# Which half of a split weight unit begins 64 bytes further: the high part instead of the low part

## The chip, the cores and the metric

The kernel runs on one core of one Trainium2 chip. The metric is the device time of one execution in microseconds (us). A core has a matrix engine (PE; its weight loads are listed apart as PEld), a vector engine (DVE), a scalar engine (ACT), GpSimd (POOL) and SyncE (SP), which issues the DMAs here. They run side by side and wait for one another through semaphores. SBUF is the working memory with 128 partitions, PSUM the memory into which PE accumulates.

## What is computed

Two layers on an input of 256 tokens by 1024 features, all in float32. Each layer is a half-weighted gated feed-forward block (FFN, 2816 hidden features), a mixer, and a second such block; an RMS norm stands ahead of each and behind each. The mixer of the first layer joins a convolution branch with a state-space branch, that of the second is an attention over three dilated windows.

```python
def swiglu(u, w1, w2):
    gate, up = jnp.split(u @ w1, 2, axis=-1)
    return (jax.nn.silu(gate) * up) @ w2
...
for i in range(DEPTH):
    g = norm_g[i]
    h = h + 0.5 * rms_norm(swiglu(rms_norm(h, g[0]), ffn_w1[i, 0], ffn_w2[i, 0]), g[1])
    u = rms_norm(h, g[2])
    ...  # m = conv_ssd_mixer(u, ...) for i = 0, dilated_attention_mixer(u, ...) for i = 1
    h = h + rms_norm(m, g[3])
    h = h + 0.5 * rms_norm(swiglu(rms_norm(h, g[4]), ffn_w1[i, 1], ffn_w2[i, 1]), g[5])
```

## The kernel before

**Weights in units.** The host cuts all weights into units of 128 partitions by 2048 float32 numbers, 1 MB each, in the order of their use. `prefetch` brings a unit into a buffer of the kind `raw` by one DMA (the first two by four), three units ahead of its use, and `split` makes two parts of it, in pieces of 512 columns: ACT writes the high part `hi` (the number rounded to the format fp32r, in which PE runs at its full rate) into a buffer of the kind `wh`, then DVE, or GpSimd for a few units, writes the low part `lo` = `raw` - `hi` into a buffer of the kind `wl`. There are four buffers each of `raw`, `wh` and `wl`. Activations are split likewise, into tiles `x` (transposed activations, both parts in one tile) and `s` (gated hidden features, one tile for each part).

**Three products.** A float32 product is made of three fp32r ones: high by high, high by low, low by high. A matmul has a stationary operand, of 128 columns, which PEld loads, and a moving operand of up to 512 columns, which streams through the array. In the profile an entry such as `w<-x,wh` names the PSUM tile that is written and the tiles that are read, without saying which is stationary.

There are three uses of a unit, and `unit(inner)` is told by `inner` how its 2048 columns are divided:

- `inner` 512 (`tok_major`): eight blocks of 128 features by 512 columns, over two units. The activation `x` is stationary, the weights move.
- `inner` 1024 (`acc_pairs`, for the second FFN product and the output projections): two blocks of 128 rows by 1024 columns. The activation (`s` or `x`) is stationary, the weights move.
- `inner` 256 (`by_parts`, `feat_major`): eight blocks of 128 features by 256 columns. Here the weights are stationary, 128 columns at a time, and the activation `x` moves.

`by_parts` makes one feature-major block in one PSUM bank of two halves. For each of eight blocks of features it issues a pair: the high weights against both parts of `x` at once (512 columns), then the low weights against the high part (256 columns, into the first half of the bank):

```python
nc.tensor.matmul(ps, w[0], x, start=kb == 0, stop=False)
nc.tensor.matmul(ps[:, 0, :], w[1], x[:, 0, :], start=False, stop=kb == KB - 1)
```

Nine of the eleven chunks of every FFN's first product go through it, and most of the attention's projections. `feat_major`, in the hybrid mixer, issues three matmuls of 256 columns for each block: high weights by high `x`, high weights by low `x`, low weights by high `x`.

**Order of the work.** The kernel is first recorded as a list of operations; `schedule` then lays them out on the engines with the costs in `cost` and the handovers between engines, gives each tile one of its kind's buffers, and `issue` emits them in that order. Costs go by engine, operation, sizes and types; addresses do not enter.

**Where buffers lie.** Before anything is issued, `lay_out` places the SBUF buffers. First come those whose size is a multiple of 512 bytes, in the order of first use, then those of the kinds with a margin; behind each of the latter, small tiles are put until its size with them reaches a multiple of 512 bytes as nearly as they can. A kind with a margin has `LINE` = 16 more columns (64 bytes) than its tiles need, and a tile's `shift` says at which column of its buffer it begins:

```python
return self.real[:, self.shift : self.shift + self.cols] if self.kind.margin else self.real
```

A matmul or a split refers to a tile through a `View`, and `placed` turns it into an address when the operation is issued; a shift therefore holds for every operation that writes or reads that tile. So far `wl` is the kind with the margin, and a unit with `inner` 256 has its low part shifted by 64 bytes. A weight unit that moves is not shifted.

Of the kernel before, what the change touches and what calls it, by code (L numbers as in the profile page):

```python
# [166 lines left out]
class View:  # L167


    def __init__(self, buf, ap, path=()):  # L170
        self.buf, self.ap, self.path = buf, ap, path
# [30 lines left out]
LINE, LINES = 16, 512  # L202
# [47 lines left out]
class Recorder:  # L250
# [11 lines left out]
    def kind(self, pool, name, count, psum=False, margin=0):  # L262
        self.kinds[name] = Kind(pool, name, count, psum, margin)
# [291 lines left out]
class Kernel:  # L555
    def __init__(self, ctx, tc, x, weights, w_dt, gains, chan, heads, dt_bias, consts, out):
        self.tc, self.nc = tc, Recorder(tc)
        self.weights, self.gains = weights, gains
        self.x, self.out = x, out
        self.n = 0  # L560
        self.next_unit = 0
        self.use_unit = 0
        self.units = {}
        self.bg = []
        nc = self.nc
        sb = ctx.enter_context(tc.tile_pool(name="sb", bufs=1))
        ps = ctx.enter_context(tc.tile_pool(name="ps", bufs=1, space=PSUM))
        kind = lambda name, count: nc.kind(sb, name, count, margin=LINE if name == "wl" else 0)
        kinds = {"raw": RAW_BUFS, "wh": W_BUFS, "wl": W_BUFS, "g": 2, "junk": 2}
        for name, count in {**kinds, **SB_BUFS, **{f"m{n}": count for n, count in SMALL.items()}}.items():  # L570
            kind(name, count)
        for name, count in PS_BUFS.items():
            nc.kind(ps, name, count, psum=True)
        self.kind = kind

        self.h = [self.keep(f"h{t}", [P, D]) for t in range(NT)]
        self.ident = self.keep("ident", [P, P])
        self.order = self.keep("order", [P, 2, P])
        self.consts = consts
        self.gain0 = self.keep("gain0", [P, KB])  # L580
        self.mhalf = self.keep("mhalf", [P, 1])
        nc.gpsimd.memset(self.mhalf, -0.5)
        self.mean = self.keep("mean", [P, P])
        nc.gpsimd.memset(self.mean, 1.0 / D)
        self.chan = self.keep("chan", [P, N_CHAN])
        self.heads = self.keep("heads", [P, 2, 16])
        self.dt_bias = self.keep("dtb", [16, 1])
        self.in_small = (chan, heads, dt_bias, w_dt)
# [46 lines left out]
    def unit(self, inner):  # L635
        i = self.use_unit
        self.use_unit += 1
        self.prefetch(i + 1 + AHEAD)
        hi, lo = self.units.pop(i)

        lo.buf.shift = LINE if inner == 256 else 0
        r = lambda a: a.rearrange("p (k n) -> p k n", n=inner)
        return r(hi), r(lo)

# [27 lines left out]
    def feat_major(self, ps, xT, unit, blk):  # L672
        hi, lo = unit
        for kb in range(KB):
            w = tuple(a[:, kb, blk * P : (blk + 1) * P] for a in (hi, lo))
            x = self.xb(xT, kb)
            mm = self.nc.tensor.matmul
            mm(ps, w[0], x[0], start=kb == 0, stop=False)
            mm(ps, w[0], x[1], start=False, stop=False)
            mm(ps, w[1], x[0], start=False, stop=kb == KB - 1)  # L680

    def by_parts(self, xT, unit, blk, bank, out, scale=1.0):

        nc = self.nc
        hi, lo = unit
        ps = self.ps([P, 2, SEQ], bank)
        for kb in range(KB):
            w = tuple(a[:, kb, blk * P : (blk + 1) * P] for a in (hi, lo))
            x = xT[kb // 2][:, kb % 2]
            nc.tensor.matmul(ps, w[0], x, start=kb == 0, stop=False)  # L690
            nc.tensor.matmul(ps[:, 0, :], w[1], x[:, 0, :], start=False, stop=kb == KB - 1)
        nc.scalar.activation(out, ps[:, 1, :], AF.Copy, scale=scale)
        if scale == 1.0:
            nc.vector.tensor_tensor(out=out, in0=ps[:, 0, :], in1=out, op=ALU.add)
        else:
            nc.vector.scalar_tensor_tensor(out=out, in0=ps[:, 0, :], scalar=scale, in1=out, op0=ALU.mult, op1=ALU.add)

    def acc_pairs(self, acc, lhs, unit, kk, start, stop, halves=(0, 1), **kw):
        hi, lo = unit
        for hf in halves:  # L700
            c = slice(hf * 512, (hf + 1) * 512)
            self.mm3(acc[hf], lhs, (hi[:, kk, c], lo[:, kk, c]), start, stop, **kw)
# [734 lines left out]
```

## Time and profile before

| | |
|---|---|
| time, median of 3 runs | 1083.91 us (1083.85 to 1084.6) |
| time of the profiled execution | 1082.94 us |
| its span, first to last instruction | 1081.2 us |
| granted TensorE clock, mean | 0.999 |
| PE busy | 1065.2 us (99%), 5822 matmuls |
| PEld busy | 903.8 us (84%), 5822 loads |
| DVE busy | 762.9 us (71%) |
| ACT busy | 656.4 us (61%) |
| read from HBM | 194.51 MB, 181 GB/s over the span |

The time is what the device needs for the whole execution, the span is what the profile sees of it. Every instruction carries the same line number (L475, where the recorder emits), so the rows are told apart by tile names. A row of the groups gives the operation, tiles, shape and count, then the busy time of the group in us, the mean duration of one in ns, and the idle time of the engine just before them. Matmuls overlap: the duration of one is longer than the distance to the start of the next, and it is the latter that adds up to the time of a stage.

### The profile page before, as it was taken

How to read it: one execution, taken by the hardware profiler on the slowest of the kernel's cores; microseconds unless marked ns; L12 is line 12 of the kernel's file. 1: busy time of each engine (PE TensorE's matmuls, PEld its weight loads, DVE VectorE, ACT ScalarE, POOL GpSimd, SP SyncE). 2: the span in 40 equal slices, each digit the busy share in tenths (PEclk: the TensorE clock that was granted, in tenths of full speed). 3: DMA queues.
4: the chain of work that ended last, by engine and by line, in shares of the span. 5: the costliest groups of instructions: out<-in, count | busy, mean ns of one | idle time of the engine just before them, and what ended most of it. 6: DMA issues, size and time to landing. Idle time of an engine off the chain costs nothing.

```text
span 1081.2 us, 15876 instructions
## 1 busy us (share of the span) xinstructions
PE 1065.2 (99%) x5822; PEld 903.8 (84%) x5822; DVE 762.9 (71%) x1572; ACT 656.4 (61%) x1449; POOL 147.3 (14%) x140
## 2 busy tenths in 40 slices
PE   7999999999999999999999999999999999999997
PEld 5888888888878888888888888888888788888886
DVE  5756666889999885765677656668688868576563
ACT  7745555787776664654565646556576756465452
POOL 2000000169896000000000000000000400000000
PEclk9999999999999999999999999999999999999999
DMA  9764465545324475546537465454745236554621
GB/s 335 283 211 178 178 202 188 164 149 195 118 92 147 190 272 195 195 159 230 175 137 273 162 228 176 175 195 145 254 158 187 98 118 214 196 195 163 227 79 39
DMA packets 30638, 196.58 MB, mean 182 GB/s; under 512 B 3680, under 2 KB 4576, under 8 KB 8032
## 3 DMA queue, kind: packets, MB, share of 16 engines
q1 hardware_dynamic: 30560, 195.57, 51.4%
q8 instruction: 45, 0.74, 0.3%
q14 instruction: 33, 0.27, 0.1%
HBM read 194.51 MB, written 1.05 MB: 181 GB/s over the span
## 4 chain that ended last, share of the span: by engine, by line
PE 93%; DVE 3%; ACT 2%; DMA 0%; issue 0%; SPq 0%; DVEq 0%; POOLq 0%; POOL 0%; ACTq 0%
PE w L475 38%; PE a L475 31%; PE t L475 12%; PE c L475 12%; DVE c L475 1%; DVE t L475 1%; ACT wh L475 1%; DMA raw<-in_weights 0%; ACT junk L475 0%; DVE s L475 0%; ACT c L475 0%; ACT t L475 0%; SPq L475 0%; DVE m L475 0%; DVE h L475 0%
## 5 line engine op out<-in xcount | busy, mean ns | idle before, releaser
L475 ACT ACTIVATE wh<-raw 128x512 fp32r<-128x512 f32 x712 | 405.4, 625 | 197.1 <-PE a L475 80.0
L475 DVE TENSOR_TENSOR wl<-raw,wh 128x512 fp32r<-128x512 f32 x640 | 412.1, 690 | 159.7 <-ACT wh L475 157.5
L475 PE MATMUL w<-x,wh 128*128 128x512 f32 (+1 forms) x864 | 266.4, 365 | 0.9 <-DVE pt L475 0.7
L475 PE MATMUL a<-wh,s 128*128 128x512 f32 x800 | 253.2, 391 | 0.0
L475 PE MATMUL w<-x,wl 128*128 128x256 f32 x752 | 210.9, 280 | 0.0
L475 PEld LDWEIGHTS w<-x,wh 128*128 128x128 f32 x864 | 154.6, 188 | 28.3 <-DVE pt L475 1.0
L475 PEld LDWEIGHTS a<-wh,s 128*128 128x128 f32 x800 | 150.0, 188 | 33.1 <-ACT s L475 0.9
L475 PE MATMUL w<-wh,x 128*128 128x512 f32 x512 | 167.1, 400 | 0.9 <-ACT x L475 0.8
L475 PE MATMUL a<-wl,s 128*128 128x512 f32 x400 | 156.6, 391 | 0.0
L475 PEld LDWEIGHTS w<-x,wl 128*128 128x128 f32 x752 | 142.9, 190 | 2.0 <-issue 0.9
L475 POOL TENSOR_TENSOR m<-m,mhalf 128x1 f32<-128x1 f32 x28 | 18.1, 647 | 801.3 <-DVE m L475 801.2
L475 PE MATMUL t<-x,wh 128*128 128x512 f32 x336 | 118.5, 392 | 0.0
L475 PE MATMUL c<-x,wh 128*128 128x512 f32 x336 | 118.5, 392 | 0.0
L475 PEld LDWEIGHTS w<-wh,x 128*128 128x128 f32 x512 | 96.0, 189 | 21.7 <-ACT x L475 1.6
L475 PE MATMUL w<-wl,x 128*128 128x512 f32 x256 | 101.9, 400 | 0.0
L475 POOL TENSOR_TENSOR wl<-raw,wh 128x512 fp32r<-128x512 f32 x72 | 90.6, 1305 | 28.1 <-ACT wh L475 27.9
L475 PE MATMUL t<-x,wl 128*128 128x256 f32 x336 | 94.0, 280 | 0.0
L475 PE MATMUL c<-x,wl 128*128 128x256 f32 x336 | 93.9, 280 | 0.0
L475 PEld LDWEIGHTS a<-wl,s 128*128 128x128 f32 x400 | 75.1, 188 | 14.7
L475 DVE TENSOR_TENSOR sg<-w,sg 128x256 f32<-128x256 f32 x72 | 30.5, 423 | 78.3 <-ACT sg L475 75.9
L475 ACT ACTIVATE sg<-w 128x256 f32<-128x256 f32 x96 | 36.7, 382 | 80.0 <-PE w L475 80.0
L475 PEld LDWEIGHTS c<-x,wh 128*128 128x128 f32 x336 | 63.1, 188 | 13.6
(176 smaller groups left out, 1202.0 us busy)
## 6 DMA issues: line engine op xcount, KB each, us to landing
raw<-in_weights SPq DMA_DIRECT2D x176, 1024.0 KB, 4.8
g<-in_gains SPq DMA_DIRECT2D x11, 512.0 KB, 5.3
raw<-in_weights SPq DMA_DIRECT2D x8, 256.0 KB, 6.2
h<-in_x SPq DMA_DIRECT2D x4, 256.0 KB, 3.1
out<-h SPq DMA_DIRECT2D x4, 256.0 KB, 2.0
g<-in_consts SPq DMA_DIRECT2D x3, 192.0 KB, 2.3
chan<-in_chan SPq DMA_DIRECT2D x1, 170.0 KB, 8.9
order<-in_consts SPq DMA_DIRECT2D x1, 128.0 KB, 8.9
```

The costliest lines, as they stand in the source:

```text
L475: o.ins = f(*[real(a) for a in o.args], **{k: real(a) for k, a in o.kw.items()})
```

## The change

The kind `wh` gets the margin in place of `wl`, and for a unit with `inner` 256 it is the high part that begins 16 columns (64 bytes) into its buffer, while the low part begins at column 0. All other tiles keep their place within their buffers; the buffers' own addresses are given out anew, since `wl` is now placed with the plain kinds and `wh` with those that have a margin.

```diff
-        kind = lambda name, count: nc.kind(sb, name, count, margin=LINE if name == "wl" else 0)
+        kind = lambda name, count: nc.kind(sb, name, count, margin=LINE if name == "wh" else 0)
...
-        lo.buf.shift = LINE if inner == 256 else 0
+        hi.buf.shift = LINE if inner == 256 else 0
```

## The prediction

> **What bounds the kernel now.** I read the page first, for the engine that sets the time.
>
> ```profile
> span 1081.2 us, 15876 instructions
> PE 1065.2 (99%) x5822; PEld 903.8 (84%) x5822; DVE 762.9 (71%) x1572; ACT 656.4 (61%) x1449; POOL 147.3 (14%) x140
> PEclk9999999999999999999999999999999999999999
> PE 93%; DVE 3%; ACT 2%; DMA 0%; issue 0%; SPq 0%; DVEq 0%; POOLq 0%; POOL 0%; ACTq 0%
> ```
>
> PE is busy for 99% of the span at a granted clock that never drops, and 93% of the chain that ended last is PE. So a nanosecond matters where a matmul starts a nanosecond later or earlier, and hardly anywhere else. The change moves bytes of the stationary weight units, so the second view is the groups of instructions by form: how many matmuls take such a unit as stationary operand?
>
> ```profile
> L475 PE MATMUL w<-x,wh 128*128 128x512 f32 x640 | 225.0, 393 | 0.0
> L475 PE MATMUL w<-x,wl 128*128 128x256 f32 x752 | 210.9, 280 | 0.0
> L475 PE MATMUL t<-x,wh 128*128 128x512 f32 x336 | 118.5, 392 | 0.0
> L475 PE MATMUL c<-x,wh 128*128 128x512 f32 x336 | 118.5, 392 | 0.0
> L475 PE MATMUL w<-x,wh 128*128 128x256 f32 x224 | 41.3, 285 | 0.9 <-DVE pt L475 0.7 <-DVE s L475 0.2
> L475 PE MATMUL a<-x,wh 128*128 128x256 f32 x96 | 17.5, 283 | 0.4 <-ACT v L475 0.4
> ```
>
> The 512-wide rows are the high products of `by_parts`: 640 + 336 + 336 = 1312. Each is followed by one 256-wide low product, so there are 1312 pairs. The 256-wide rows with `wh`, 224 + 96 = 320, are the two high products of `feat_major`; with one low product each two, that is 160 triples.
>
> What one pair costs is not its "mean ns" (matmuls overlap), but the distance from start to start. The chain of waits in order of time gives it; its columns are start us, us, what:
>
> ```profile
> 46.58 10.93 PE a L475 x48
> 57.50 5.55 PE w L475 x32
> ```
>
> The second row is 16 pairs in 5.55 us: 346.9 ns a pair, and 1312 x 346.9 ns = 455 us, 42% of the span. The first row is a run of 512-wide matmuls whose stationary operand is an activation and starts at the buffer's beginning, both parts: 10.93 / 48 = 227.7 ns each. Now the timeline of PE inside both runs (start us, us, instruction):
>
> ```profile
> 46.41 0.40 PE L475 MATMUL a<-wh,s 128*128 128x512 f32 x1
> 46.65 0.40 PE L475 MATMUL a<-wl,s 128*128 128x512 f32 x1
> 46.88 0.62 PE L475 MATMUL a<-wh,s 128*128 128x512 f32 x2
> 47.34 0.39 PE L475 MATMUL a<-wl,s 128*128 128x512 f32 x1
> 47.58 0.40 PE L475 MATMUL a<-wh,s 128*128 128x512 f32 x1
> ...
> 56.44 0.62 PE L475 MATMUL a<-wh,s 128*128 128x512 f32 x2
> 56.89 0.39 PE L475 MATMUL a<-wl,s 128*128 128x512 f32 x1
> 57.12 0.39 PE L475 MATMUL a<-wh,s 128*128 128x512 f32 x1
> 57.34 0.39 PE L475 MATMUL w<-x,wh 128*128 128x512 f32 x1
> 57.57 0.28 PE L475 MATMUL w<-x,wl 128*128 128x256 f32 x1
> 57.69 0.40 PE L475 MATMUL w<-x,wh 128*128 128x512 f32 x1
> 57.92 0.28 PE L475 MATMUL w<-x,wl 128*128 128x256 f32 x1
> 58.03 0.39 PE L475 MATMUL w<-x,wh 128*128 128x512 f32 x1
> 58.26 0.28 PE L475 MATMUL w<-x,wl 128*128 128x256 f32 x1
> 58.38 0.39 PE L475 MATMUL w<-x,wh 128*128 128x512 f32 x1
> ```
>
> Two things are to be seen. The plain 512-wide stream starts at (47.58 - 46.41) / 5 = 234 ns a matmul and ends at (57.34 - 56.44) / 4 = 225 ns; the whole run's 227.7 says that most of it is near 227. So the same instructions with the same addresses modulo a buffer run at 234 when they come out of a `by_parts` run and then settle. And a pair divides into 230 ns from high to low (0.23, 0.23, 0.23) and 117 from low to high (0.12, 0.11, 0.12). The load of the next stationary operand runs under each matmul: today the shifted low load under the long matmul, the unshifted high load under the short one. The change swaps the two.
>
> **The change part by part.** The planner's `cost` has no term for a margin or a shift, so the order, the instructions, the waits and the DMAs stay as they are, on all queues; only addresses change. There are four effects.
>
> (1) The buffers of `wh` grow by 64 bytes and those of `wl` shrink. `lay_out` starts every large buffer at the same remainder of 512 bytes and fills the rest of each enlarged one with small tiles; it does so with the other kind too. Price 0; below and above there is nothing to bound it by but the other prices.
>
> (2) ACT writes the high part, DVE or GpSimd reads it 64 bytes further on, and writes the low part at the beginning.
>
> ```profile
> L475 DVE TENSOR_TENSOR wl<-raw,wh x640: 676/684/1584, 8.9 to 1058.5; 128x512 fp32r<-128x512 f32 x160
> L475 ACT ACTIVATE wh<-raw x712: 612/622/718, 8.2 to 1057.8; 128x512 fp32r<-128x512 f32 x178
> ACT wh L475 <- PE a L475: 80.0, 37, 3.2
> ```
>
> The DVE row mixes shifted outputs (units used as stationary) with unshifted ones, and its shortest and median are 8 ns apart, so a shifted operand costs at most about 8 ns of 684. The cover is the prefetch: splits wait for a free buffer, that is for PE (80.0 us in 37 waits in the last row), not the other way round. Were the cover gone, 640 x 8 ns = 5 us would be the most. I take 0.
>
> (3) The triples, 160 of them, get two shifted loads instead of one. They stand in the hybrid stage, where the chain is not on PE; for the window from 224 to 260 us it says:
>
> ```profile
> by line: DVE c L475 44.9%; DVE t L475 32.4%; DVE s L475 9.6%; DVE m L475 3.8%; DVE cv L475 3.6%; ACT c L475 2.6%; DVE a L475 2.1%; PE w L475 1.1%; issue 0.7%
> ```
>
> DVE's long convolution sets the end there and hides the triples. Without that cover, 3 ns on each of 480 matmuls would be 1.4 us in either direction. I take 0.
>
> (4) The pairs. No row has an unshifted low load under the long `x` stream, or a shifted high load under a short matmul in a pair, so both halves are bounded by neighbours. From high to low, now 230: the unshifted load under a 512-wide stream took 227 settled and 234 unsettled. Lower end -3, upper end +4; the pair's alternation of long and short never gives a plain stream to settle in, nor a change of stream, behind which 234 was seen, so it lies between, and I take the middle, 230.5: +0.5. From low to high, now 117: the loads' own durations (min/median/max) bound it. The first row is of the window 225 to 259 us, where the low load runs under a 256-wide matmul, the others are of the whole span.
>
> ```profile
> L475 PEld LDWEIGHTS w<-x,wl x80: 189/192/192, 224.9 to 255.7; 128*128 128x128 f32 x80
> L475 PEld LDWEIGHTS c<-x,wl x336: 187/189/193, 43.6 to 1058.0; 128*128 128x128 f32 x168
> L475 PEld LDWEIGHTS c<-x,wh x336: 186/188/188, 43.5 to 1057.9; 128*128 128x128 f32 x168
> ```
>
> A shifted load takes up to 192 ns, an unshifted one 188. If the short matmul hides none of that, the step is +4. Whether it hides it, the triples show, start to start:
>
> ```profile
> 225.17 0.40 PE L475 MATMUL w<-x,wh 128*128 128x256 f32 x2
> 225.41 0.28 PE L475 MATMUL w<-x,wl 128*128 128x256 f32 x1
> 225.52 0.40 PE L475 MATMUL w<-x,wh 128*128 128x256 f32 x2
> ...
> 226.23 0.40 PE L475 MATMUL w<-x,wh 128*128 128x256 f32 x2
> ```
>
> (226.23 - 225.17) / 9 = 117.8 ns a matmul, although one in three has the 192 ns load under it; that is 0.8 above the pair's 117. So I take +0 here, with ends -1 (a shifted load that hurries the short step) and +4.
>
> The Trainium skill ("TensorE: Matmul & The Clock Gate", LDWEIGHTS) states that a weight load takes the number of its columns over 1.2, in ns, thus 107 for 128 columns; the same page gives a warm 256-wide matmul 256 / 2.4 + 2.5 = 109, an estimate from its figures. By these two the load is as long as the short matmul and the 4 ns would all be exposed: +5.2 us in place of 0. The triples' 117.8 do not bear that out, hence it is a rival and not the sum.
>
> Sum: +0.5 ns x 1312 pairs = +0.7 us, all else 0. The profiled execution took 1082.94 us, 1.74 more than its span, and the median of the runs shown is 1083.91, 0.97 above it. 1083.91 + 0.7 = 1084.6 us. 2.2 us (0.2%) is about what a measurement of this kernel can tell from no change; that is 1.65 ns a pair.
>
> **The rivals.** *A: the low load collides (slower).* Unshifted, it runs under the long matmul as in the unsettled stream, 234 for 230, and the alternation keeps it from settling. For it: the same 512-byte remainders as in the 234 ns rows. Against: that stream does settle within its run. Price +4 x 1312 = +5.2 us: 1089.1. It decides from 231.7 on.
>
> *B: the high load's last 4 ns show under the short matmul (slower).* For it: loads of 192 ns exist only where a shift is. Against: the triples' 117.8. Price between half (today only about half of the pairs' shifted loads are long, median 189) and all: +2 to +4 ns x 1312 = +2.6 to +5.2 us: 1086.5 to 1089.1. With A it would reach 1094.
>
> *C: the long step settles to the plain stream's 227 and the short one stays at 117 (faster, the other side).* For it: that stream's settled rows are the nearest unshifted loads under a 512-wide matmul. Against: their moving operand is a weight, not `x`. Price -3 x 1312 = -3.9 us: 1080.0. It decides from 228.3 downwards.
>
> That the change does nothing it says can be left out: the shift belongs to the buffer and is applied when instructions are issued, so the split writes where the matmuls read.
>
> **How the numbers follow.** My forecast, a pair within 1.65 ns of today's, gets 0.40; A 0.21, B alone 0.14, C 0.25. Hence slower 0.35, same 0.40, faster 0.25. The likeliest one's own range is 1081.7 to 1086.1. For 8 in 10 I go to C with its short step at -1 as well as its 3 ns, 4 x 1312 = 5.2 below the median: 1078.7, taken as 1079; and above to A with half of B, 6 x 1312 = 7.9 us: 1091.8, taken as 1092. Outside stay A with all of B and a settling faster than any row here.
>
> **What would show it.** In the profile after, 16 pairs in the chain of waits should again take 5.5 to 5.6 us. The load's durations should change places: `wh` loads of up to 192, `wl` loads of 188. From high to low near 230 confirms (4); 234 is A, 227 is C; from low to high of 119 to 121 is B. Splits should stay at 622 and 684 ns. Pairs at 340 or 353 ns would mean that the two steps depend on each other, so that bounding each by itself, as done in (4), was the error.

## The result, and the profile after

The changed kernel takes 1076.99 us (median of 4 runs, 1076.7 to 1077.57), the kernel before 1083.88 in the runs beside it: a ratio of 0.9938, 95% interval 0.992 to 0.9955. It is 0.6% faster. The forecast was 1084.6 us, no change, and the time lies below its range.

The page after:

```profile
span 1074.9 us, 15876 instructions
PE 1058.9 (99%) x5822; PEld 897.9 (84%) x5822; DVE 762.3 (71%) x1572; ACT 654.9 (61%) x1449; POOL 147.4 (14%) x140
PE 93%; DVE 3%; ACT 2%; DMA 0%; issue 0%; SPq 0%; DVEq 0%; POOLq 0%; POOL 0%; ACTq 0%
```

The span is 6.3 us shorter, PE's busy time too (1065.2 to 1058.9), with the same 5822 matmuls and the same shares in the chain. So the matmuls start closer together. The chain of waits in order of time (start us, us, what), after:

```profile
57.47 5.46 PE w L475 x32
62.93 2.72 PE t L475 x16
65.65 2.72 PE c L475 x16
68.37 5.46 PE a L475 x24
```

and the same stretch before:

```profile
57.50 5.55 PE w L475 x32
63.05 2.77 PE t L475 x16
65.82 2.77 PE c L475 x16
68.60 5.49 PE a L475 x24
```

A row of 32 is 16 pairs: 5.46 / 16 = 341 ns where it was 347; a row of 16 is 8 pairs: 2.72 / 8 = 340. A chunk of 32 pairs falls from 11.09 to 10.90 us. (A wide stream is a run of 512-wide matmuls in which the weights move, such as the row of 24.) Each FFN has eight such chunks behind its first wide stream of second products, four FFNs 32 of them: 32 x 0.19 = 6.1 us. The 24 wide streams between these chunks fall from 5.49 to 5.46 us each, some 0.7 us in all, and the pairs in other places lose about as much, as shown below; together that is nearly all of the gain. The timeline of PE after shows where in a pair:

```profile
57.31 0.40 PE L475 MATMUL w<-x,wh 128*128 128x512 f32 x1
57.55 0.28 PE L475 MATMUL w<-x,wl 128*128 128x256 f32 x1
57.66 0.39 PE L475 MATMUL w<-x,wh 128*128 128x512 f32 x1
57.89 0.28 PE L475 MATMUL w<-x,wl 128*128 128x256 f32 x1
58.00 0.39 PE L475 MATMUL w<-x,wh 128*128 128x512 f32 x1
58.23 0.28 PE L475 MATMUL w<-x,wl 128*128 128x256 f32 x1
```

After a first 0.24 the long step takes 0.23 each time and the short one 0.11. The starts in the trace, which has whole nanoseconds, give medians of 227 and 113 ns in this chunk, against 230 and 117 before: **both** steps became shorter. Not every run of pairs gained. The first chunk of an FFN starts behind transposes, not behind a wide stream; in all four FFNs it became slower, in the first 2.80 us for 8 pairs (350 ns) where it was 2.77 before, and so did most of the attention's pairs. Here is the first FFN's first chunk, after and before:

```profile
36.73 4.20 PE w L475 x24
40.93 2.80 PE t L475 x16
```

```profile
36.86 4.17 PE w L475 x24
41.03 2.77 PE t L475 x16
```

So the same instructions, with operands at the same remainders of 512 bytes, repeat with 340 ns in one run and 350 ns in another. Such a spacing, which holds from the start of a run to its end, is called a cycle below.

### The profile page after: what moved, and what is told of

The parts are those of the page before. It is cut to its first block, busy times and chain, and to the rows that moved or that the text cites. A ratio compares the mean times of both kernels' runs of the same rounds, so it can differ in the third digit from the quotient of the medians.

```text
span 1074.9 us, 15876 instructions
## 1 busy us (share of the span) xinstructions
PE 1058.9 (99%) x5822; PEld 897.9 (84%) x5822; DVE 762.3 (71%) x1572; ACT 654.9 (61%) x1449; POOL 147.4 (14%) x140
## 4 chain that ended last, share of the span: by engine, by line
PE 93%; DVE 3%; ACT 2%; DMA 0%; issue 0%; SPq 0%; DVEq 0%; POOLq 0%; POOL 0%; ACTq 0%
PE w L475 38%; PE a L475 32%; PE t L475 12%; PE c L475 12%; DVE c L475 2%; DVE t L475 1%; ACT wh L475 1%; DMA raw<-in_weights 0%; ACT junk L475 0%; DVE s L475 0%; ACT c L475 0%; ACT t L475 0%; SPq L475 0%; DVE m L475 0%; DVE h L475 0%
```

## The experiments

The theories are stated in the expectations, numbered from 1 to 5; the later ones came when the earlier had fallen. Each was timed beside the kernel before on the same chip; ratios are to it. The pairs are read from the second chunks of the first FFN, in the chain of waits between 57 and 70 us.

**No shift at all, and where the buffers lie.** Two kernels shift nothing; one keeps the margin on `wh`, the other on `wl`, so that their buffers lie as in the changed kernel and as in the one before.

```diff
-        hi.buf.shift = LINE if inner == 256 else 0
+        hi.buf.shift = 0
```

> Margin on wh as in the changed kernel, but no part of a stationary unit is shifted. Theory 1 (each step by itself: the cost of a matmul depends on whether the load under it begins 64 bytes off the moving operand's remainder; long step 227 ns over an unshifted load and 230 over a shifted one, short step 117 over an unshifted and 113 over a shifted one): pair 227 + 117 = 344 ns, 1312 x 4 ns = 5 us slower than the changed kernel, about 1082 us. Theory 2 (what matters is that the high and the low load lie apart from each other; the pair locks as a whole): pair about 350 ns, as in the changed kernel's runs that start behind a break, 13 us slower than the changed kernel, about 1090 us. Theory 3 (where the buffers lie, not the shift): about 1077 us.

> Margin on wl as in the kernel before, no part of a unit shifted. Theories 1 and 2: equal to the kernel with the margin on wh and no shift, within 2 us, because the placing of the buffers does not matter. Theory 3 (where the buffers lie): equal to the kernel before, about 1084 us, and 6 to 7 us slower than the one with the margin on wh.

They took 1091.75 us (ratio 1.0066, 1.0049 to 1.0082) and 1091.49 us (1.0067, 1.0052 to 1.0082). Margin on `wh`, then on `wl`:

```profile
42.71 2.77 PE t L475 x16
...
59.18 5.64 PE w L475 x32
```

```profile
58.14 5.64 PE w L475 x32
```

Both need 5.64 / 16 = 352.5 ns a pair. The placing of the buffers does nothing (theory 3 falls). Theory 1 falls too: its 227 + 117 gave 344. The time fits theory 2. The row at 42.71 is of the first chunk, and there this kernel without a shift takes 2.77 us for 8 pairs, as the kernel before does. So the spacing of the kernel before is found without any shift too; what is missing is one of 340 ns.

**Both parts shifted.** Margins on both kinds; an unused tile goes out to make room.

```diff
         hi.buf.shift = LINE if inner == 256 else 0
+        lo.buf.shift = hi.buf.shift
```

> Both parts of a stationary unit are shifted by 64 bytes (margins on both kinds; an unused tile and its memset are left out to make room, small tiles lie elsewhere). Theory 1 (each step by itself): long step 230, short step 113, pair 343 ns, 4 us slower than the changed kernel, about 1081 us. Theory 2 (apart from each other): same as no shift at all, about 350 ns a pair and 1090 us.

1091.76 us (1.0073, 1.0058 to 1.0088), and again:

```profile
58.10 5.64 PE w L481 x32
```

As slow as no shift; theory 1's 343 ns is off by 10. One part of the two has to be shifted, and not the other.

**How far.** The distance of the high part is changed, `LINE` from 16 columns (64 bytes) to 8, 24, 32, 48 and 64 columns.

```diff
-LINE, LINES = 16, 512
+LINE, LINES = 64, 512
```

> The changed kernel with 32 bytes in place of 64. If the two loads have to lie in different pieces of 64 bytes: partly as no shift, 347 to 353 ns a pair, 1084 to 1092 us. If any distance does it: 340 ns, 1077 us.

> The changed kernel with 96 bytes in place of 64. With the period of 128 bytes that 128, 192 and 256 showed, 96 is 32 on the other side of 64: if 64 is the best point and its sides are alike, about 351 ns a pair and 1089 us as with 32 bytes; if more than 64 is as good as 64, 340 ns and 1077 us.

> The changed kernel with 128 bytes in place of 64. Theory 2 (the distance of the high load from the low load decides) with a period of 128 bytes: as with no shift, 352.8 ns a pair and about 1091.7 us. With a period of 256 bytes: neither 0 nor 64; the high part lies as far ahead of the low part as behind it, so between the two kernels at the worst, 340 to 347 ns, 1077 to 1084 us.

> The changed kernel with 192 bytes in place of 64. Period 256 bytes: 192 ahead is 64 behind, so this is the kernel before in another place, 346.9 ns a pair and about 1084 us. Period 128 bytes: 192 is 64, so 340 ns and about 1077 us; the kernel before would then have to be explained by something else than the distance.

> The changed kernel with 256 bytes in place of 64. Theory 1 with a fine grain (any offset off the moving operand's remainder of 512 does it): 340 ns a pair, 1077 us. If the offset must be small, because the load is to begin just behind or ahead of the moving stream: 344 to 350 ns a pair, 1082 to 1090 us.

| bytes | time us | ratio (95%) |
|---|---|---|
| 32 | 1088.91 | 1.0045 (1.003 to 1.006) |
| 64 (the change) | 1076.99 | 0.9938 (0.992 to 0.9955) |
| 96 | 1084.04 | 1.0005 (0.9996 to 1.0014) |
| 128 | 1090.64 | 1.0059 (1.0042 to 1.0076) |
| 192 | 1077.1 | 0.9936 (0.9922 to 0.9951) |
| 256 | 1091.63 | 1.0069 (1.0054 to 1.0084) |

A chunk's first row for 32, 96, 128, 192 and 256 bytes, one kernel a fence:

```profile
58.59 5.62 PE w L475 x32
```

```profile
57.41 5.55 PE w L475 x32
```

```profile
59.01 5.62 PE w L475 x32
```

```profile
58.46 5.46 PE w L475 x32
```

```profile
58.09 5.64 PE w L475 x32
```

192 is as good as 64, 128 and 256 are about as bad as 0. What counts is the remainder of 128 bytes, and 64 is the best point tried; 32 and 96 would be alike if the two sides of 64 were; they are not (5.62 and 5.55). With this period, 64 ahead and 64 behind are the same distance, so theory 2 alone cannot tell the changed kernel from the one before. Something third must be in it.

**The moving operand's place.** The high part is shifted in every unit, also where the weights move and activations are stationary.

```diff
-        hi.buf.shift = LINE if inner == 256 else 0
+        hi.buf.shift = LINE
```

> The changed kernel with the high part shifted in every unit, also where it is the moving operand (inner 512 and 1024). Theory 2: the moving operand's place does not matter, so those 512-wide streams stay at 227 ns, the pairs at 340 ns, and the time at 1077 us. Theory 1 in its remaining form (place of the load against the moving operand): two in three of some 2060 wide matmuls change by 3 ns, 4 us either way.

1091.72 us (1.0073, 1.0058 to 1.0088):

```profile
46.65 11.20 PE a L475 x48
57.85 5.45 PE w L475 x32
68.74 5.59 PE a L475 x24
74.33 5.60 PE w L475 x32
...
85.53 5.60 PE a L475 x24
91.13 5.45 PE w L475 x32
```

The wide stream of 48 takes 11.20 / 48 = 233 ns a matmul where the kernel before has 10.93 / 48 = 228. No load was moved there, only two in three moving operands, so the place of the moving operand matters. The pairs, whose addresses are those of the changed kernel, need 340 ns behind one stream (5.45) and 350 behind the next (5.60), and 340 again behind a stream that is like that one (5.59 and 5.60). So these addresses allow both cycles. A cycle stays through a chunk, although its 32 pairs go through two units and several PSUM tiles; this speaks for the beginning of a run as what chooses, but what in the beginning it is, the runs do not show.

**The activations shifted instead.** Now `x`, the moving operand of the pairs, is shifted by 64 bytes as well, once in the kernel before (low part shifted) and once in the changed one.

```diff
-        return [self.slot([P, 2, 2, SEQ], F32R, "x") for _ in range(KB // 2)]
+        tiles = [self.slot([P, 2, 2, SEQ], F32R, "x") for _ in range(KB // 2)]
+        for v in tiles:
+            v.buf.shift = LINE
+        return tiles
```

> The kernel before (low part shifted) with every tile of x shifted by 64 bytes too (margins on wl and x, an unused tile and its memset left out). Against the moving operand x the high load is then 64 off and the low load is not, as in the changed kernel. Theory 4 (remainder modulo 128 of a load against the operand that moves above it: the long step wants the same remainder, the short step one 64 off): 340 ns a pair in the runs behind a wide stream. The wide streams with x stationary are now 64 off, as the ones in the kernel with the high part shifted everywhere, 233 for 227 ns: 864 x 6 ns = 5 us more; in all about 1082 us. Theory 5 (only the two loads against each other, high one ahead): 347 ns a pair as in the kernel before, about 1089 us.

> The changed kernel with every tile of x shifted by 64 bytes too. Against x the high load is then not off and the low load is, as in the kernel before. Theory 4: 347 ns a pair, and 5 us more in the wide streams with x stationary, about 1089 us. Theory 5: 340 ns a pair as in the changed kernel, about 1082 us with the wide streams' 5 us, 1077 without.

Low part and `x` shifted: 1079.53 us (0.996, 0.9945 to 0.9975). High part and `x` shifted: 1089.34 us (1.0052, 1.0035 to 1.0069). In this order:

```profile
30.05 5.60 PE w L484 x24
...
58.06 5.46 PE w L484 x32
```

```profile
29.51 5.60 PE w L484 x24
...
57.79 5.60 PE w L484 x32
...
798.46 5.55 PE w L484 x32
```

This settles it against theory 5; theory 4 has the right kernel short, but not the other one's 347 ns. With `x` shifted, the roles change over: shifting the low part now gives 340 ns, and shifting the high part gives 350. The distance of the two parts is the same in both; what differs is which load has the same remainder as the operand that moves above it. The pairs are short where the load under the long matmul has the same remainder as `x` and the load under the short one is 64 bytes off. The first row of each fence is a wide stream with `x` stationary, 24 in 5.60 us; before it was

```profile
29.40 5.48 PE w L475 x24
```

so there, too, 64 off costs 5 ns a matmul. That is a reason why the first of the two is not as fast as the changed kernel although its pairs are; theory 4's 1082 us was 2.5 us too high. The second has the offsets of the kernel before but repeats at 350 and not at 347 ns, except in some runs of the attention (the row at 798.46, 347 ns): this set of offsets, too, has more than one cycle.

The cycle of 340 ns belongs to one set of offsets alone. In the traces of the four kernels in which the high load is 64 bytes off `x` and the low load is not (the changed one, 192 bytes, the high part shifted in every unit, the low part and `x` shifted), runs of pairs settle at 340 ns. In the other eleven kernels no eight pairs in a row take less than 346 ns a pair.

**Half-way places.** `x` by 32 and the high part by 96 bytes, then `x` by 96 and the high part by 32. The high load stays 64 off `x`, the low one is 32 off on one side and on the other.

```diff
-            v.buf.shift = LINE
+            v.buf.shift = 8
...
-        hi.buf.shift = LINE if inner == 256 else 0
+        hi.buf.shift = 24 if inner == 256 else 0
```

> Tiles of x shifted by 32 bytes and the high part by 96. Against x the high load is 64 off as in the changed kernel, the low load 96 (32 on the other side), and in the wide streams the stationary x is 32 off the moving weights. Theory 4 with a grain of 64 bytes: the long step is neither same nor 64 off, so between 227 and 233 ns, and the short step stays at 113: 342 to 347 ns a pair; wide streams with x stationary between 227 and 233 ns. If 32 off were better than the same remainder, they would fall below 227 ns, which would open a way to a faster kernel.

> Tiles of x shifted by 96 bytes and the high part by 32. Against x the high load is 64 off, the low load 32, the stationary x of the wide streams 96 off. Theory 4: as with the roles of 32 and 96 exchanged, 342 to 347 ns a pair; wide streams with x stationary between 227 and 233 ns, below 227 if this offset is better than none.

1091.26 us (1.007, 1.0047 to 1.0093) and 1089.86 us (1.0055, 1.0033 to 1.0078):

```profile
29.22 5.60 PE w L484 x24
...
57.54 5.62 PE w L484 x32
```

```profile
29.92 5.61 PE w L484 x24
...
58.19 5.59 PE w L484 x32
```

5.62 and 5.59 us are 351 and 349 ns a pair, worse than the 342 to 347 expected. The long step's load is best at the same remainder, of the places tried; moving it by 32 either way loses the short cycle. The wide streams with `x` stationary say the same (the rows at 29 us): 5.60 and 5.61 us for 24, 233 to 234 ns a matmul, so 32 off costs as much there as 64 off. No kernel here is faster than the changed one by more than the intervals; the one with 192 bytes is its equal.

## Why the prediction was wrong

**The bound and the count held.** PE set the time, 1312 pairs were the main place of weight, and most of the gain is found in 1024 of them.

**(1), (2) and (3) held.** Where buffers lie was worth nothing (1091.75 against 1091.49 us without a shift). The splits stayed at 622 and, after, 685 ns:

```profile
L475 DVE TENSOR_TENSOR wl<-raw,wh x640: 677/685/1577, 8.9 to 1052.2; 128x512 fp32r<-128x512 f32 x160
L475 ACT ACTIVATE wh<-raw x712: 612/622/723, 8.3 to 1051.6; 128x512 fp32r<-128x512 f32 x178
```

The triples cost nothing, though the reason given covers only a part of them: the window from 224 to 260 us holds 289 of their 480 matmuls, and for some of the others PE is on the chain. One such stretch, 38 of their matmuls, took nearly the same before and after:

```profile
283.67 4.76 PE a L475 x38
```

```profile
281.91 4.74 PE a L475 x38
```

**(4) failed, and with it the sum.** Its step was to bound the long and the short step each by itself, from neighbouring streams, and to add. The forecast was +0.5 and 0 ns, the lower ends -3 and -1, a pair of 343; measured are -3 and -4, a pair of 340. (The unsettled 234 was read from rounded starts; whole nanoseconds give 232 for those five matmuls, which would have lowered the upper end and changed nothing else.) The long step did what rival C said, 227. The short step fell to 113, below the end of 116, with a shifted load under it; so rival B's price did not appear, nor the +5.2 us for all of the load's last 4 ns. The trace before had 113 ns, in 256-wide matmuls with loads of 16 columns, which had not been taken as an end; the timeline of PE before:

```profile
222.30 0.28 PE L475 MATMUL w<-x,wdtl 128*16 128x256 f32 x1
...
223.32 0.28 PE L475 MATMUL w<-x,wdtl 128*16 128x256 f32 x1
```

Nine matmuls start from the first row to the last: (223.32 - 222.30) / 9 = 113 ns. The deeper fault is the adding: with the steps as measured, the same rule gives 344 ns for no shift and 343 for both shifts, and both cost 353. The two steps repeat as one cycle. The prediction named 340 or 353 as the sign of just that, but gave it no chance.

**The loads' durations were a false guide.** Long loads were to move with the shift. In the hybrid stage they did, `wl` from 192 to 188 and some of `wh` to 192 (the first two rows, after, 223 to 257 us). In the pairs nearly all vanished (the last two, whole span):

```profile
L475 PEld LDWEIGHTS w<-x,wl x80: 187/188/189, 223.2 to 253.9; 128*128 128x128 f32 x80
L475 PEld LDWEIGHTS w<-x,wh x159: 186/188/192, 223.1 to 253.8; 128*128 128x128 f32 x159
...
L475 PEld LDWEIGHTS c<-x,wh x336: 186/188/189, 43.5 to 1051.6; 128*128 128x128 f32 x168
L475 PEld LDWEIGHTS c<-x,wl x336: 187/188/192, 43.6 to 1051.7; 128*128 128x128 f32 x168
```

The shifted `wh` load takes at most 189 ns under the short matmul. Nor does a load of 192 need a shift: in the kernel with the margin on `wl` and nothing shifted, loads of the hybrid stage have it too, while the kernel with both parts shifted, at 353 ns a pair, has nearly none (in this order):

```profile
L475 PEld LDWEIGHTS a<-x,wl x48: 188/192/192, 253.2 to 295.9; 128*128 128x128 f32 x48
```

```profile
L481 PEld LDWEIGHTS c<-x,wl x336: 187/188/190, 44.2 to 1066.5; 128*128 128x128 f32 x168
```

So the loads' durations tell neither the shift nor the cycle, and rival B's premise, that 192 exists only where a shift is, was wrong.

**Rival A's long step came in a part of the pairs.** In this kernel's first chunk in the first FFN the long step has a median of 233 ns in the trace, and in the second chunk of the kernel without a shift (margin on `wh`) one of 236, although the low load under it lies at the same remainder as in the runs at 227. So the low load's place does not set the long step by itself. In the wide streams 233 ns appear once load and moving operand are 64 off. That is the opposite of the condition that was given for A: the same remainder is the good place under the matmuls of a wide stream.

**What was not foreseen at all** is that one set of addresses has several cycles, so that a part of the pairs, as in the first chunk above, became slower. How far the time falls therefore depends also on how many pairs find the cycle of 340 ns: most of them here, but only about a third with the high part shifted in every unit, where the pairs have the same offsets. Why there are several cycles, what chooses among them, and which machinery sets the 128 bytes, the runs do not show.

## What to carry to other kernels

Where PE sets the time and weight loads alternate with matmuls, the byte address of a stationary operand, taken modulo 128 against the operand that moves while it is loaded, is worth trying: here 340 to 353 ns a pair, 1.4% of the whole time, with no instruction changed. Do not add up steps from neighbouring streams; read the length of the whole repeating cycle, for each kind of beginning. And give a step that repeats a thousand times the shortest value seen for its shape anywhere in the trace as the lower end.

## What the runs showed of the hardware

The spacing of 512-wide fp32r matmuls settles at 227 ns where load and moving operand have the same remainder of 128 bytes, and at 233 where they are 64 apart (11.20 us against 10.93 for 48) or 32 (5.60 against 5.48 for 24). A 256-wide matmul with a full load of 128 columns took 113 ns in the best cycle, as long as one with a load of 16, and 117 in the kernel before. The Trainium skill ("TensorE: Matmul & The Clock Gate", Part 2, the step on LDWEIGHTS) says that "Loading the next tile's weights doesn't steal SBUF read bandwidth from the running matmul." These runs do not bear that out as a rule on time: the same loads and matmuls cost up to 4% more by their addresses alone (353 against 340 ns a pair). Whether reading SBUF is the reason, they do not show.
